# A hybrid decoder step: the mLSTM chunk steps regrouped, decode key gathers in a job of their own, the start's loads reordered

## The chip, the cores and the metric

The kernel runs on one core of a Trainium2 chip. The metric is device time in microseconds for one execution of the whole program; below, TensorE, VectorE, ScalarE, GpSimd and SyncE are PE, DVE, ACT, POOL and SP in the profile's rows, and SP's rows are mostly the DMAs that it issues.

## The reference

One layer of a decoder step, for 1024 prompt tokens (S) and 8 decode tokens (NB), which are handled together as R = 1032 columns of x. What is computed:

```python
h = RMSNorm(x) * norm_w                      # x: 1032 x 2048
aq,ak,av, iq,ik,iw, az, mq,mk,mv, mi,mf, mo,mz = split(h @ w_in)
# prompt attention: the indexer selects the 256 best earlier keys for each query
score[t,s] = sum_h relu(iq[t,h] . ik[s]) * iw[t,h]
att[t]     = softmax over top-256 keys of aq . ak, times av          # 8 heads, 2 KV heads
# decode attention: the same over 4096 cached keys in pages, 256 of them gathered for each of 8 rows
# mLSTM, 4 heads, q and k 128 wide, v 256 wide, chunk by chunk:
s   = (q k^T) * d                            # d = exp(log_d - m_t), causal
num = a * (C q) + s v ;  den = a * (n . q) + sum(s)
h_t = num / max(|den|, exp(-m_t))
C   = a_end * C + sum_s w[s] v[s] k[s]^T ;  n likewise
out = RMSNorm(x + concat(att * silu(az), norm(h_ml) * sigmoid(mo) * silu(mz)) @ w_out)
```

Everything is float32. Outputs are the normed result, the new keys and values, and the mLSTM state for prompt and decode.

## The kernel before, in words

**Projection.** TensorE's main work is h @ w_in, as 61 tiles of up to 128 output columns by 1032 tokens (`proj`, matmuls at L1333). Tile 0 (`T_MISC`, 88 columns) holds the small paths, 1 to 8 are the indexer's queries, then follow k, v and q of attention, q, k and v of mLSTM (25 to 36), the gates of mLSTM (`T_G` = 37 to 52) and of attention (`T_AZ` = 53 to 60). A float32 factor is split into a high and a low part of a type that TensorE takes at full rate (wH, wL by L210 on ScalarE and L211 on VectorE; xH, xL by L261 and L262), and three products replace one: H·H, H·L, L·H. A tile goes in four quarters of four k blocks of 128 rows; with three chunks of 344 tokens a quarter is 4 x 3 x 3 = 36 matmuls. After the fourth quarter `evac` empties the PSUM banks (L329, into `ev` buffers, six in all), scales by the row's rstd, and does what the path needs: for a gate tile a Sigmoid on ScalarE and a product on GpSimd (L371), for tiles below `T_G` a copy of the 8 decode columns into `dec` on GpSimd (L332). After the projection comes the product with w_out (L1470).

**The start.** Tiles 0, 1 and 2 run together, so that x, which is loaded block by block (16 blocks of 128 x 1032, `xr`), is used three times on its arrival. `xbegin` loads block 0 in three chunks and the first quarter of the three tiles' weights, in two parts: k = 0, and k = 1 to 3. `xload(k)` loads each further block, splits it and adds its squares to `acc`. `xhook` calls these ahead of tile 0's matmuls of each quarter. In a quarter the order of weights and x is tile 0's weights, four blocks of x, and then tiles 1 and 2's weights; those of quarter 1 are pinned.

**Lanes.** All else is cut into small pieces placed between the quarters. Two lanes each run a list of jobs; a job is a generator whose `yield` gives a cost. `Lane.step`, called after each quarter, runs pieces until the job's cost is spread evenly up to its due tile. Lane 0: `gates`, `index`, `att` (prompt attention), `ml` (mLSTM of the prompt). Lane 1: `dscore`, `dsel`, `datt` (decode attention), `dml` (mLSTM of decode). A job's line has its first tile, its due tile and its weight:

```python
Job("ml", T_G, T_PRE, 36, job_ml)
```

**Order.** Each engine carries out its instructions in the order that a scheduler gives them; it follows dependences and priorities (weights and evacuations are high), and what is wrapped in `pin` keeps its place in the program's order. SP issues most DMAs, so a load that waits for its buffer holds those behind it in SP's order. Pools give each named tile `bufs` buffers.

**mLSTM steps (`job_ml`).** 16 steps: 8 chunks of 128 tokens by two pairs of heads. For each step `load` fetches q and k (`qk`), v (`vT`, L779) and two rows for each head (`rb`, L783, four DMAs that broadcast a row of `rowS`). `prep` copies the decay's last column (`dk`, L789), forms d = exp of the masked difference on VectorE and ScalarE (L797 is the Exp), scales q, then has on TensorE the scores (L802), with d multiplied at L803, split into dH and dL (`split`, L769 and L770), the transposes of k (L806), scaled and split again (ksH at L769), and those of v, split into aH and aL (L814, L815). `main` does the products: state times q and scores times v (L828 on), the state's update (L832), and the norm of the heads. `tail` transposes the heads (L862, of `hm` from L854) and stores them. The loop runs `main(n)` and the loads of step n + 2, then a quarter of the projection, then `prep(n + 1)` and `tail(n)`, then a quarter. The first `prep` comes three quarters after the first loads.

**Decode attention (`job_datt`).** For each of 8 rows GpSimd gathers 2 x 128 keys by an indirect DMA (`kv`, L1181, a pool of six buffers in the job), two rows ahead of use; VectorE multiplies them by q (`jk`, L1209) and sums. After the softmax the values are gathered in the same way, two rows ahead, and multiplied on TensorE (L1254), eight passes a row, one row to a piece of cost 2500.

**Prompt attention (`job_att`).** At the end of each half of a group's heads the sums of exponentials are transposed, copied into a tile `rt` and stored to `rcS`, which the evacuations of the `T_AZ` tiles read. `rt` takes the single buffer named `ob`, which holds attention outputs too.

Of the kernel before, what the change touches and what calls it, by code (L numbers as in the profile page):

```python
# [8 lines left out]
F32 = mybir.dt.float32  # L9
# [10 lines left out]
NB = 8  # L20
# [117 lines left out]
def body(tc, A, stop=None):  # L138
# [126 lines left out]
    def xbegin():  # L265
        xr = x0.tile([128, R], F32, name="xr")
# [3 lines left out]
        one, rest = slice(0, 1), slice(1, 4)  # L270
        pin(SY.dma_start(nw, A["nw"]))
        for _, _, load, _ in ws:
            pin(load(one, SC))
        pin(SC.activation(warm, mhalf, AF.Square))
        for c in range(3):
            pin(SY.dma_start(xr[:, cs[c]], A["xT"][0, :, cs[c]]))
        for _, _, load, _ in ws:
            pin(load(rest))
        spin(14)
        todo = [lambda c=c: xsplit(0, xr, cs[c]) for c in range(3)]  # L280
        cast = [w[3] for w in ws]
        for f in (lambda: cast[0](one), todo[0], lambda: cast[1](one), lambda: cast[2](one), todo[1], todo[2],
                  lambda: cast[0](rest), lambda: cast[1](rest), lambda: cast[2](rest)):
            a, v = f()
            pin(a)
            pin(v)
        pin(SC.activation(acc, xr, AF.Square))
# [233 lines left out]
    def job_att():  # L521
# [3 lines left out]
        with tc.tile_pool(name="at", bufs=2) as pa:  # L525
# [126 lines left out]
            for n, pair in enumerate(pairs):  # L652
# [103 lines left out]
    def job_ml():  # L756
        gT = mlc["gT"]
        with tc.tile_pool(name="ml", bufs=2) as pm:
# [28 lines left out]
            def prep(c, h0, qk, vT, rb):  # L787
                dk = pm.tile([128, 2], F32, name="dk")
                V.tensor_copy(dk, rb[:, 1, :, 127])  # L789
                d = pm.tile([128, 2, 128], F32, name="d")  # L790

                def col(x):
                    return gT[:, x, h0 * 8 + c:(h0 + 1) * 8 + c + 1:8].unsqueeze(2).to_broadcast([128, 2, 128])

                pin(V.tensor_tensor(d, rb[:, 0], col(0), OP.subtract))
# [3 lines left out]
                V.tensor_tensor(qt, qk[:, 0:2], rb[:, 1], OP.mult)  # L799
                pS = bank().rearrange("p (a b) -> p a b", a=4)  # L800
                for hh in range(2):
                    PE.matmul(pS[:, hh, :], qk[:, 2 + hh, :], qk[:, hh, :], start=True, stop=True)  # L802
                V.tensor_tensor(d, pS[:, 0:2], d, OP.mult)  # L803
                dH, dL = split(d, "d")
                for hh in range(2):
                    PE.transpose(pS[:, 2 + hh, :], qk[:, 2 + hh, :], ident)  # L806
                ks = pm.tile([128, 2, 128], F32, name="ks", bufs=1)
                V.tensor_tensor(ks, pS[:, 2:4], col(1), OP.mult)
                kH, kL = split(ks, "ks")
                pv = bank().rearrange("p (a b) -> p a b", a=2)  # L810
                for x in range(4):
                    PE.transpose(pv[:, x // 2, (x % 2) * 128:(x % 2) * 128 + 128], vT[:, x, :], ident)
                aH, aL = (pm.tile([128, 2, 258], F32R, name=f"a{x}", bufs=1) for x in "HL")
# [54 lines left out]
            ld = [load(*steps[0]), load(*steps[1])]  # L868
            yield 1
            yield 1  # L870
            yield 1
            cur = prep(*ld.pop(0))
            yield 1
            for n in range(len(steps)):
                mid = main(*cur)
                if n + 2 < len(steps):
                    ld.append(load(*steps[n + 2]))
                yield 1
                if n + 1 < len(steps):
                    cur = prep(*ld.pop(0))  # L880
                tail(*mid)
                yield 1
# [186 lines left out]
    def job_dml():  # L1069
        with tc.tile_pool(name="dm", bufs=1, side="right") as pd:  # L1070
# [9 lines left out]
            yield 2000  # L1080
            yield 2000
            yield 2000
# [23 lines left out]
            yield 2000  # L1106
            yield 2000
# [53 lines left out]

    def job_datt():
        with tc.tile_pool(name="da", bufs=1, side="right") as pd:
# [13 lines left out]
            def gather(src, b):  # L1177
                out = []
                for u in range(2):
                    g = pd.tile([128, 256], F32, name="kv", bufs=6)  # L1180
# [3 lines left out]
                    if not u:  # L1184
                        pin(gi)
# [15 lines left out]
            for b in range(NB):  # L1201
                if b + 2 < NB:
                    kgs.append(gather("ck", b + 2))
# [352 lines left out]
```

## Time and profile before

| what | value |
|---|---|
| median of 3 runs | 2077.87 us (2075.32 to 2081.95) |
| the profiled execution | 2064.6 us, its span 2062.8 us |
| PE | 2034.1 us busy, 99% of the span |
| PE weight loads (beside the matmuls) | 1999.7 us, 97% |
| DVE | 1215.2 us, 59% |
| ACT | 836.4 us, 41% |
| POOL | 331.5 us, 16% |
| HBM | 131 GB/s over the span |

The span is that of one profiled execution; its own time is 1.8 us more. A busy TensorE also holds the time in which it runs at a lower clock, so the share alone does not tell how fast it went; the granted clock stands in a row of its own. In rows of waits the columns are the engine and its operation, what released it, the sum of the waits in us, their number, and the longest. In rows of the timeline they are the start, the duration in us, engine, line, operation, and in brackets the idle time ahead and what ended it. In rows by windows they are the window, its length, busy time (and count) of PE, PE weight loads, DVE, ACT and POOL, the granted clock (1 is full), the share of the DMA engines, and GB/s. In rows of groups they are the busy time and the mean in ns, and behind the bar the idle time ahead of them and its releaser.

### The profile page before, as it was taken

How to read it: one execution, taken by the hardware profiler on the slowest of the kernel's cores; microseconds unless marked ns; L12 is line 12 of the kernel's file. 1: busy time of each engine (PE TensorE's matmuls, PEld its weight loads, DVE VectorE, ACT ScalarE, POOL GpSimd, SP SyncE). 2: the span in 40 equal slices, each digit the busy share in tenths (PEclk: the TensorE clock that was granted, in tenths of full speed). 3: DMA queues.
4: the chain of work that ended last, by engine and by line, in shares of the span. 5: the costliest groups of instructions: out<-in, count | busy, mean ns of one | idle time of the engine just before them, and what ended most of it. 6: DMA issues, size and time to landing. Idle time of an engine off the chain costs nothing.

```text
span 2062.8 us, 36440 instructions
## 1 busy us (share of the span) xinstructions
PE 2034.1 (99%) x13284; PEld 1999.7 (97%) x13284; DVE 1215.2 (59%) x3060; ACT 836.4 (41%) x1667; POOL 331.5 (16%) x405
## 2 busy tenths in 40 slices
PE   8999999999999999999999999989999999999997
PEld 8999999999999999999999999989999999999997
DVE  8332457556695876886455455356676467374464
ACT  8122244233531455312365555434454235343343
POOL 0002556600000000024011001012222111101011
PEclk9999999999999999999999999999999999999998
DMA  7444533322222212254322332256665758586584
GB/s 244 106 110 116 157 108 113 107 75 72 78 68 74 72 59 71 63 168 136 107 75 86 107 98 70 72 158 190 189 198 161 190 194 273 150 249 182 148 256 138
DMA packets 229777, 272.85 MB, mean 132 GB/s; under 512 B 36661, under 2 KB 162741, under 8 KB 229597
## 3 DMA queue, kind: packets, MB, share of 16 engines
q1 hardware_dynamic: 222381, 256.70, 42.0%
q0 software_dynamic: 5632, 12.59, 2.2%
q8 instruction: 104, 1.70, 0.4%
q10 hardware_dynamic: 1584, 1.23, 0.2%
q14 instruction: 76, 0.62, 0.1%
HBM read 210.54 MB, written 59.88 MB: 131 GB/s over the span
## 4 chain that ended last, share of the span: by engine, by line
PE 88%; DMA 4%; DVE 3%; ACT 1%; issue 1%; SPq 1%; POOL 0%; DVEq 0%; ACTq 0%; POOLq 0%
PE pj L1333 56%; PE bank L1470 17%; PE bank L441 3%; PE bank L636 2%; PE bank L585 2%; PE bank L627 2%; PE bank L935 1%; PE bank L1333 1%; DMA qk<-mlS 1%; DMA xr<-in_xT_dram 1%; DMA ev<-gateS 0%; DMA out_C_s_dram<-Cb 0%; PE bank L1053 0%; DVE wL L211 0%; DMA rb<-rowS 0%
## 5 line engine op out<-in xcount | busy, mean ns | idle before, releaser
L1333 PE MATMUL pj<-xH,wH 128*128 128x344 f32 (+2 forms) x2736 | 883.5, 324 | 6.3 <-ACT xH L261 3.2
L1333 PE MATMUL pj<-xL,wH 128*128 128x344 f32 (+2 forms) x2736 | 883.2, 323 | 0.2 <-DVE xL L262 0.2
L1333 PE MATMUL pj<-xH,wL 128*128 128x344 f32 (+2 forms) x2736 | 882.9, 323 | 0.0
L210 ACT CAST wH<-wraw 128x512 fp32r<-128x512 f32 (+2 forms) x439 | 267.6, 614 | 636.1 <-PE pj L1333 429.4
L1333 PEld LDWEIGHTS pj<-xH,wH 128*128 128x128 f32 (+1 forms) x2736 | 513.5, 188 | 10.6 <-ACT xH L261 4.8
L1333 PEld LDWEIGHTS pj<-xL,wH 128*128 128x128 f32 (+1 forms) x2736 | 513.4, 188 | 3.0 <-DVE xL L262 1.0
L1333 PEld LDWEIGHTS pj<-xH,wL 128*128 128x128 f32 (+1 forms) x2736 | 513.9, 188 | 2.0
L211 DVE TENSOR_TENSOR wL<-wraw,wH 128x512 fp32r<-128x512 f32 (+2 forms) x439 | 305.5, 700 | 350.6 <-ACT wH L210 338.3
L1470 PE MATMUL bank<-mH,wH 128*128 128x388 f32 (+1 forms) x768 | 245.0, 321 | 0.4 <-ACT wH L210 0.4
L1470 PE MATMUL bank<-mL,wH 128*128 128x388 f32 (+1 forms) x768 | 244.9, 319 | 0.0
L1470 PE MATMUL bank<-mH,wL 128*128 128x388 f32 (+1 forms) x768 | 244.4, 319 | 0.0
L922 POOL DMA_INDIRECT kp<-in_cik_dram,idx x128 | 128.6, 1005 | 105.6 <-PE bank L935 56.3
L1470 PEld LDWEIGHTS bank<-mH,wH 128*128 128x128 f32 x768 | 144.3, 188 | 0.7 <-ACT wH L210 0.6
L1470 PEld LDWEIGHTS bank<-mL,wH 128*128 128x128 f32 x768 | 144.5, 188 | 0.0
L1470 PEld LDWEIGHTS bank<-mH,wL 128*128 128x128 f32 x768 | 144.2, 188 | 0.0
L490 ACT ACTIVATE eq<-eq 128x512 bf16<-128x512 bf16 (+2 forms) x93 | 78.4, 843 | 113.7 <-DVE eq L489 113.4
L443 ACT ACTIVATE rl<-bank 128x512 f32<-128x512 f32 (+2 forms) x160 | 79.0, 522 | 79.5 <-PE bank L441 51.9
L446 DVE SCALAR_TENSOR_TENSOR s<-rl,wiN,s 128x512 f32<-128x512 f32 (+2 forms) x150 | 94.9, 654 | 21.5 <-ACT rl L443 18.4
L329 DVE TENSOR_TENSOR ev<-pj,rstd 128x344 f32<-128x344 f32 x144 | 73.6, 512 | 53.7 <-PE pj L1333 44.9
L632 DVE TENSOR_TENSOR ptL<-bank,ptH 128x512 fp32r<-128x512 f32 (+1 forms) x80 | 50.5, 635 | 64.3 <-ACT ptH L631 63.7
L1480 POOL TENSOR_TENSOR acc<-acc,sq 128x388 f32<-128x388 f32 (+1 forms) x42 | 43.1, 1025 | 280.3 <-ACT sq L1478 280.3
L332 POOL COPY dec<-ev 128x8 f32<-128x8 f32 x28 | 11.4, 406 | 475.9 <-DVE ev L329 198.9
(367 smaller groups left out, 2441.6 us busy)
## 6 DMA issues: line engine op xcount, KB each, us to landing
wraw<-in_wa_dram SPq DMA_DIRECT2D x238, 256.0 KB
wraw<-in_wo_dram SPq DMA_DIRECT2D x192, 256.0 KB
gateS<-ev SPq DMA_DIRECT2D x72, 172.0 KB
mlS<-ev SPq DMA_DIRECT2D x48, 172.0 KB
xr<-in_xT_dram SPq DMA_DIRECT2D x15, 516.0 KB
mL<-gateS SPq DMA_DIRECT2D x32, 194.0 KB
xr<-in_xT_dram SPq DMA_DIRECT2D x32, 194.0 KB
out_yT_dram<-y SPq DMA_DIRECT2D x32, 194.0 KB
```

What stands on the lines that cost most here:

```text
L210: a = SC.copy(H[:, s, :cols], raw[:, s, :cols])
L211: return a, V.tensor_tensor(L[:, s, :cols], raw[:, s, :cols], H[:, s, :cols].bitcast(F32), OP.subtract)
L329: V.tensor_tensor(e, ps[c][:cols, :cn], rstd[:cols, c0:c0 + cn], OP.mult)
L441: PE.matmul(p[:, :cn], qi[:, h % 4, :], ki[x][:, c0:c0 + cn], start=(x == 0), stop=(x == 1))
L443: SC.activation(r[:, :cn], p[:, :cn], AF.Relu)
L446: v = V.scalar_tensor_tensor(s[:, c0:c0 + cn], r[:, :cn], wv, s[:, c0:c0 + cn], OP.mult, OP.add)
L490: SC.activation(junk2[:, :W1], junk2[:, :W1], AF.Copy, accum_out=cnt[:, 1:2])
L632: V.tensor_tensor(pL[:, :kw], pt[:, :kw], pH[:, :kw].bitcast(F32), OP.subtract)
L922: g = G.indirect_dma_start(out=kp, out_offset=None, in_=A["cik"], in_offset=bass.IndirectOffsetOnAxis(ap=idx[:, m:m + 1], axis=0))
L1333: PE.matmul(ps[:cols, :cn], w_[:, k, :cols], x_[kk][:, c0:c0 + cn], start=(kk == 0 and z == 0), stop=(kk == 15 and z == 2))
L1470: PE.matmul(p, w_[:, k, :], x_, start=(n == 0), stop=(n == 47))
L1480: G.tensor_tensor(acc, acc, sq, OP.add)
```

## The change

Four parts; the projection, the indexer and the output product stay.

- **mLSTM steps.** `prep` is cut in two: `decay` (dk, d, Exp, scaled q) and `prep` (the three kinds of TensorE work first, the splits behind them). `decay` of a step runs one step ahead of its `prep`, loads run three steps ahead, the first `prep` comes after five quarters of waiting, and `tail(n)` moves to the piece after `prep(n + 1)`, ahead of `main(n + 1)`. `dk` is pinned. `dml` waits one piece longer at two places.
- **Decode gathers.** The gathers of keys go into a job `rows` of lane 1 ahead of `datt`, with a pool of 16 buffers; those of the values follow one row behind the use of the keys. A row of value products costs 1500 in place of 2500.
- **Attention's row sums** are copied into a buffer of the six named `pP` and no longer into `ob`.
- **The start.** Weights of quarter 0 come in three parts (k = 0, k = 1, k = 2 and 3), x of k = 1 is loaded ahead of the second part and split by `xbegin`; of the later loads of x only k = 2 is pinned; for quarter 1 tile 0's weights are pinned, and those of tiles 1 and 2 are not.

The due tile of `att` goes from 48 to 47.75 and some weights follow.

```diff
 def xbegin():
-        xr = x0.tile([128, R], F32, name="xr")
+        xr = [x0.tile([128, R], F32, name="xr") for k in range(2)]
...
-        one, rest = slice(0, 1), slice(1, 4)
+        parts = slice(0, 1), slice(1, 2), slice(2, 4)
...
+        pin(SY.dma_start(xr[1], A["xT"][1]))
+        for s in parts[1:]:
+            for w in ws:
+                pin(w[2](s))
         spin(14)
...
+        both(xsplit(0, xr[0], cs[2]))
+        for w in ws:
+            both(w[3](parts[1]))
+        both(xsplit(1, xr[1], slice(0, R)))
+        add(0, acc)
+        for w in ws:
+            both(w[3](parts[2]))
+        add(1, x0.tile([128, R], F32, name="sq", bufs=2))
...
 def xload(k):
-        if k < 4:
+        if k == 2:
             pin(dma)
...
 # job_att
-                    rt = pa.tile([128, 2, 128], F32, name="ob", bufs=1)[:32, 0]
+                    rt = pa.tile([128, 512], F32, name="pP", bufs=6)[:32, :128]
...
 # job_ml
-            def prep(c, h0, qk, vT, rb):
+            def decay(c, h0, qk, vT, rb):
                 dk = pm.tile([128, 2], F32, name="dk")
-                V.tensor_copy(dk, rb[:, 1, :, 127])
+                pin(V.tensor_copy(dk, rb[:, 1, :, 127]))
...
+                return c, h0, qk, vT, dk, d, qt
+
+            def prep(c, h0, qk, vT, dk, d, qt):
...
             ld = [load(*steps[0]), load(*steps[1])]
+            for _ in range(5):
+                yield 1
+            dcs = [decay(*ld.pop(0))]
             yield 1
+            cur = prep(*dcs.pop())
+            ld.append(load(*steps[2]))
+            dcs = [decay(*ld.pop(0))]
             yield 1
-            yield 1
-            cur = prep(*ld.pop(0))
-            yield 1
+            mid = None
             for n in range(len(steps)):
+                if mid:
+                    tail(*mid)
                 mid = main(*cur)
-                if n + 2 < len(steps):
-                    ld.append(load(*steps[n + 2]))
+                if n + 3 < len(steps):
+                    ld.append(load(*steps[n + 3]))
                 yield 1
                 if n + 1 < len(steps):
-                    cur = prep(*ld.pop(0))
-                tail(*mid)
-                yield 1
+                    cur = prep(*dcs.pop())
+                    if n + 2 < len(steps):
+                        dcs = [decay(*ld.pop(0))]
+                    yield 1
+            tail(*mid)
...
+    def job_rows():
+        rowctx.pool = rowctx.enter_context(tc.tile_pool(name="kvp", bufs=1, side="right"))
+        yield 1
+        for b in range(NB):
+            kgs.append(gather("ck", b))
+            yield 1
...
 # job_datt
             for b in range(NB):
-                if b + 2 < NB:
-                    kgs.append(gather("ck", b + 2))
+                if b:
+                    vgs.append(gather("cv", b - 1))
...
-            vgs = [gather("cv", b) for b in range(2)]
+            vgs.append(gather("cv", NB - 1))
...
-                if b + 2 < NB:
-                    vgs.append(gather("cv", b + 2))
...
-                yield 2500
+                yield 1500
...
+                   Job("rows", T_AK, 35.5, NB + 1, job_rows),
...
 # proj, xhook
-                        ws.append(wsplit(wsrc(t, q), cols, x0, 2, 4, q == 1))
+                        ws.append(wsplit(wsrc(t, q), cols, x0, 2, 4))
...
-            ws.append(wsplit(wsrc(0, q), NMISC, wst, 2, 3, q == 1))
+            ws.append(wsplit(wsrc(0, q), NMISC, wst, 2, 3, True))
...
-        for k in range(max(1, q * 4), q * 4 + 4):
+        for k in range(max(2, q * 4), q * 4 + 4):
             xload(k)
```

More of the change, by code (lines that the diff above doesn't have):

```diff
@@ L1176, in job_datt @@
             lT = pd.tile([128, 2, 64], F32, name="lT")
[L1177 to L1180, printed above, removed]
-                    gi = G.indirect_dma_start(out=g, out_offset=None, in_=A[src],
-                                         in_offset=bass.IndirectOffsetOnAxis(ap=idxs[:, b, u:u + 1], axis=0))
-                    out.append(g)
-                    if not u:
-                        pin(gi)
-                return out
             def qload(b):
```

78 lines of the change are left out of this document (46 added, 32 removed).

## The prediction

> **What bounds the kernel now.** The page comes first: spans and busy shares by engine, then the granted clock by slice.
>
> ```profile
> span 2062.8 us, 36440 instructions
> ...
> PE 2034.1 (99%) x13284; PEld 1999.7 (97%) x13284; DVE 1215.2 (59%) x3060; ACT 836.4 (41%) x1667; POOL 331.5 (16%) x405
> ...
> PEclk9999999999999999999999999999999999999998
> ```
>
> TensorE is busy for 2034.1 of 2062.8 us. The change removes and adds no matmul: the built programs hold the same number of each kind. So it can only move what TensorE loses: 28.7 us of idle time, and stretches at a lower clock, which count as busy. The second view is the list of waits, for PE alone: in total, times, the longest.
>
> ```profile
> PE pj L1333 <- ACT xH L261: 3.2, 3, 1.5
> PE bank L806 <- DVE d L803: 2.7, 2, 2.6
> PE pj L1333 <- DVE ev L329: 2.4, 2, 1.6
> PE bank L862 <- DVE hm L854: 2.0, 2, 1.1
> ...
> PE bank L1333 <- ACT wH L210: 0.8, 1, 0.8
> ...
> PE bank L832 <- ACT ksH L769: 0.6, 1, 0.6
> PE bank L1254 <- DMA kv<-in_cv_dram,idxs: 0.5, 2, 0.4
> ```
>
> L261 and L210 belong to the start, L806, L862 and L832 to the mLSTM steps, L1254 to decode attention; L329 is the evacuation of a projection tile. These 12.2 us are all that the change can aim at, beside clock losses.
>
> The third view is the timeline at these places, with one row of the chain that ended last as the yardstick, and the clock by windows.
>
> ```profile
> 1614.32 66.34 PE pj L1333 x422
> ```
>
> An undisturbed projection matmul takes 66.34 / 422 = 0.157 us.
>
> ```profile
> 977.04:980.45 3.41, 2.88 (x21) 2.31 (x20) 0.00 (x0) 0.00 (x0) 2.78 (x3) 1.00 0.41 124
> 980.50:983.90 3.40, 3.40 (x14) 3.40 (x14) 0.00 (x0) 0.47 (x1) 1.91 (x3) 0.53 0.33 92
> 1349.20:1352.60 3.40, 0.84 (x7) 0.67 (x6) 1.93 (x6) 0.69 (x2) 0.99 (x2) 1.00 0.25 30
> 1352.70:1355.80 3.10, 3.10 (x13) 3.10 (x13) 1.37 (x5) 0.34 (x2) 0.00 (x0) 0.51 0.94 263
> 981.14 0.49 PE L1333 MATMUL pj<-xL,wH 128*128 128x344 f32 x1
> ...
> 983.72 0.49 PE L1333 MATMUL pj<-xL,wH 128*128 128x344 f32 x1
> ```
>
> The column after the POOL count is the granted clock. It stood at 0.53 and 0.51 in two stretches of some 3.4 us, each behind a stretch of that length in which PE did little. Between the last two rows nine matmuls start in 2.58 us, 0.287 each instead of 0.157. Eleven in such a stretch: 11 x 0.130 = 1.4 us lost, twice.
>
> **The change part by part.** Working is against the profiled execution: 2064.6 us, its span and 1.8 around it. The median of the three runs, 2077.87, lies 13.3 us above; I take that as constant and subtract the same microseconds from it.
>
> *The start.* Three places:
>
> ```profile
> 4.89 0.65 ACT L210 CAST wH<-wraw 128x128 fp32r<-128x128 f32 x2
> ...
> 9.85 1.15 ACT L261 ACTIVATE xH<-xr,nw 128x1032 fp32r<-128x1032 f32 x1 [0.89 <-DMA xr<-in_xT_dram]
> 11.05 0.70 PE L1333 MATMUL pj<-xH,wH 128*88 128x344 f32 x3 [1.52 <-ACT xH L261]
> 27.35 0.70 PE L1333 MATMUL pj<-xH,wH 128*88 128x344 f32 x3 [0.90 <-ACT xH L261]
> 28.81 0.44 PE L1333 MATMUL bank<-xH,wH 128*128 128x388 f32 x1 [0.76 <-ACT wH L210]
> 4.00:8.00 4.00, 2.95 (x16) 2.07 (x15) 2.89 (x8) 3.31 (x9) 0.00 (x0) 1.00 1.04 319
> ```
>
> At 9.85 ScalarE waits for x of k = 1, which was queued behind three quarters of the first weights. The change queues it ahead of them, and puts a k = 1 part of 176 KB before the rest. So 352 KB less (three quarters of 704 KB make 528; 176 stay) lie ahead of k = 1's work; at 319 GB/s of the last row that is 1.1 us. The wait of 1.52 falls to 0.4. The casts of that part (three of 0.65 / 2, some 0.3 us) then run in ScalarE's idle 0.89. At 27.35 and 28.81 TensorE had nothing but the 88-column tile for k = 4 to 7: the other two tiles' second weights were issued behind x of k = 7. In the changed program's SP order both stand ahead of x of k = 4, and PE's order takes 21 matmuls for each k instead of 9, so 21 x 0.157 = 3.3 us cover each x load. Of 0.90 + 0.76 = 1.66 I take 1.2 away. Together -2.3; at best -3.2. The bound on the other side: the Square of x0 now stands behind the split of x1 (1.15 us), and x3's load waits for that buffer: +1.2.
>
> *Attention's row sums in another buffer.* Two copies at the end of a head group no longer wait for the ob buffer. No wait for them is in the list of PE; the transposed sums go to DRAM and are read tiles later. Nothing; were they late, their reader is the gate stage, some 30 us on.
>
> *Decode attention.* Key gathers go ahead of it, in a job of their own, on 16 buffers instead of 6, and value gathers follow one batch row behind, so GpSimd stops waiting for VectorE there:
>
> ```profile
> POOL kv L1181 <- DVE jk L1209: 32.6, 16, 3.0
> 917.39 0.39 PE L1333 MATMUL pj<-xH,wH 128*128 128x344 f32 x1 [0.76 <-DVE ev L329]
> 969.75 2.73 PE L1254 MATMUL bank<-PT,kv 128*128 128x4 f32 x24
> ```
>
> The wait at 917.39 is an evacuation behind jk work; that work keeps its size, so I count half: -0.4. Gathers queued on GpSimd wait for the index list; behind them stand the dec copies, which hold one evacuation buffer of six, used by three chunks a tile: covered. The value matmuls (L1254) lose the wait of 0.5 for gathers, and the slow stretch after 980.5 (1.4): -1.9. But with all values there, the changed order holds all 64 passes without a projection matmul among them. At 2.73 / 24 = 0.114 us that is 7.3 us in which the array streams four columns at a time. The 24 of before brought no lower clock; the mixed stretch from 977.04, with PE at 2.88 of 3.41, did. Bounds: nothing, or half the clock from 3.4 us on: 3.9 us of passes become 7.8, and 1.4 are lost behind them: +5.3. I take half, 2.6, nearest to the row from 977.04. Net +0.7; with the evacuation, +0.3.
>
> [...]
>
> *The mLSTM steps.*
>
> ```profile
> 1333.71 0.50 SPq L783 DMA_DIRECT2D rb<-rowS  x1
> ...
> 1335.68 0.90 SPq L783 DMA_DIRECT2D rb<-rowS  x2
> ...
> 1341.62 0.34 DVE L789 COPY dk<-rb 128x2 f32<-128x2 f32 x1 [5.50 <-DMA rb<-rowS]
> 1343.10 0.43 PE L1333 MATMUL pj<-xH,wH 128*128 128x344 f32 x1 [1.64 <-DVE ev L329]
> 1350.67 0.17 DVE L789 COPY dk<-rb 128x2 f32<-128x2 f32 x1 [5.59 <-DMA rb<-rowS]
> 1351.93 0.44 PE L806 MATMUL bank<-cst,qk 128*128 128x128 f32 x2 [2.56 <-DVE d L803]
> ...
> 1345.00:1600.00 255.00, 249.63 (x1660) 245.79 (x1659) 166.07 (x561) 116.10 (x250) 55.71 (x102) 0.99 0.63 178
> ```
>
> VectorE, in order, stands 5.5 us at a row load, twice; the evacuation behind the first, and the score product d behind the second, hold TensorE. The change loads three steps ahead, gives five quarters (of 36 matmuls, 5.7 us) instead of three before the first, and takes decay a step ahead of its products. SP issued the first step's four rb rows from 1333.7 to 1336.6, two quarters before use; with two quarters more, 11 us, these waits end. The transposes of k stand before d now, so L806's wait cannot occur. Heads are transposed (L862) after two quarters and the products between them, not one and some: 2.0 goes. L832's 0.6 came of the late d. Sum: 1.6 + 2.7 + 2.0 + 0.6 + 1.4 of clock = 8.3. The gates of decode's mLSTM share VectorE in the first steps, and a first wait for rb may stay: I take -7.0; from -8.3 to -2.
>
> The price: the order has 62 activation table loads, not 46, as Exp of decay falls between the Sigmoids of gates.
>
> ```profile
> L797 ACT ACT_TABLE_LOAD x8 | 10.3, 1283 | 0.3 <-DMA gateS<-ev 0.2
> L803 DVE TENSOR_TENSOR d<-bank,d 128x256 f32<-128x256 f32 x16 | 6.7, 419 | 7.4 <-PE bank L802 7.4
> L769 ACT CAST dH<-d 128x256 fp32r<-128x256 f32 x16 | 6.5, 406 | 11.8 <-DVE d L803 11.8
> L770 DVE TENSOR_TENSOR dL<-d,dH 128x256 fp32r<-128x256 f32 x16 | 6.9, 430 | 0.0
> L815 DVE TENSOR_TENSOR aL<-bank,aH 128x512 fp32r<-128x512 f32 x16 | 11.0, 684 | 0.3
> L211 DVE TENSOR_TENSOR wL<-wraw,wH 128x512 fp32r<-128x512 f32 x35 | 26.5, 757 | 18.3 <-ACT wH L210 16.1 <-DMA gateS<-ev 2.2
> L329 DVE TENSOR_TENSOR ev<-pj,rstd 128x344 f32<-128x344 f32 x24 | 12.1, 508 | 7.9 <-POOL ev L371 4.3 <-PE pj L1333 3.5
> ```
>
> 16 x 1.283 = 20.5 us of ScalarE. Cover: between a step's transposes and its products lie 36 matmuls, 5.7 us. The chain in them is d 0.42, dH 0.41, dL 0.43, the same three for the keys, and aL 0.68: 3.2 us, with one weight split (0.76) 4.0. One load more makes 5.2, below 5.7. So hidden; for places where an evacuation joins, +0.5, up to +17 (below).
>
> **Sum.** -2.3 + 0.3 - 7.0 + 0.5 = -8.5. Profiled: 2056.1; median: 2069.4.
>
> **Rivals.** *Clock and start* (2074): the value batch costs its full 5.3, so decode gives +5.3 - 1.9 - 0.4 = +3.0, and the start gives back what it gains, because loads are the bound there (DMA share 1.04 in its row). 0 + 3.0 - 7.0 + 0.5 = -3.5. For it: the two clock rows; against: the 24 passes at full clock.
>
> *The waits only move* (2074): VectorE still meets rows that have not landed, as SP queues them between weight loads that wait for buffers; the first steps keep 6 of 8.3 us. -2.3 + 0.3 - 2.3 + 0.5 = -3.8. That the program is not what the edit says is excluded by its order: 36 matmuls stand between every two parts.
>
> *Table loads in the steps* (2085): where a gate's evacuations fall into the cover, the chain is 4.0 + three evacuations (1.5) + a load (1.3) = 6.8, 1.1 us over 5.7; with 0.3 for the evacuation behind, TensorE loses 1.4. In 12 of 16 steps that is 16.8: -2.3 + 0.3 - 7.0 + 16.8 = +7.8. It decides from 11 steps on (15.4 - 9.0 = +6.4). For it: ScalarE's order puts Exp between two Sigmoids of one tile. Against: of before's waits in such steps the list has none for aL or kL, and evacuations come once in four quarters.
>
> **Chances.** Forecast case 0.66, clock and start 0.13, waits move 0.10, table loads 0.11. A measurement of this kernel can tell some 0.3%, 6 us, about the spread of its three runs. Faster takes in the forecast case down to -6.2, 0.62 in all; the rest of it and the two small gains are the same: 0.27; table loads slower: 0.11. The range goes from all gains at best (start -3.2, decode -0.8 - 1.9, mLSTM -8.3: -14.2, some 2063.5, so 2063) to no change and a little, 2080, which takes in both small rivals; above it lies the table case, below it little.
>
> **What would show it.** In the changed profile: L261 and L210 gone from PE's waits before 30 us; no dk wait over 1 us; PE idle between 1345 and 1600 under 1.5 us instead of 255.0 - 249.6 = 5.4; granted clock below 1 only around the 64 passes. Wrong would be: PE waiting for aH, dL or ksH in many steps, evacuations late by more than 1 us in the gate stage, or a slow clock elsewhere.

## The result, and the profile after

The changed kernel takes 2084.70 us (median of 20 runs, 2083.11 to 2090.55), the kernel before beside it 2079.59 us (20 runs, 2074.26 to 2087.15): a ratio of 1.0029, 95% interval 1.0020 to 1.0037. By the ratio it is slower by some 6 us (5.1 us by the medians), where 8.5 us less had been forecast.

The page of the changed kernel, its span and the busy shares:

```profile
span 2086.0 us, 36465 instructions
...
PE 2045.0 (98%) x13284; PEld 2007.8 (96%) x13284; DVE 1212.2 (58%) x3063; ACT 859.4 (41%) x1686; POOL 332.8 (16%) x405
```

TensorE has the same 13284 rows. Beside the first profile of before it is busy for 10.9 us more (2045.0 against 2034.1) and idle for 41.0 us instead of 28.7. But that profile is of an execution of 2064.6 us, and beside the changed kernel before takes 2079.59 us. Nearer to that is the third profile of before (under Experiments), of an execution of 2077.55 us and a span of 2075.7 us:

```profile
PE 2037.4 (98%) x13284; PEld 1999.6 (96%) x13284; DVE 1214.7 (59%) x3060; ACT 837.1 (40%) x1667; POOL 330.0 (16%) x405
```

Against it the changed kernel's span is 10.3 us longer: PE is busy for 7.6 us more, at a mean granted clock of 0.992 instead of 0.996, and idle for 2.7 us more. So most of the loss is a lower clock. The waits of PE in the changed kernel (total, times, longest):

```profile
PE pj L1369 <- DVE ev L346: 7.7, 6, 2.7
PE pj L1369 <- DVE gi L1117: 7.7, 1, 7.7
...
PE bank L251 <- DVE rstd L253: 1.6, 2, 0.8
...
PE pj L1369 <- ACT xH L261: 1.1, 2, 0.7
```

The lines have moved by some 36: L1369 is the projection, L346 the evacuation. Of the waits of before, those for d, hm, ksH, wH and the value gathers are gone, and 1.1 us for xH is left. In their place stand one of 7.7 us behind gi, which is decode's mLSTM, and more late evacuations. Where the clock went is in the timeline and in the windows:

```profile
10.77 0.49 PE L1369 MATMUL pj<-xL,wH 128*88 128x344 f32 x1
11.05 0.49 PE L1369 MATMUL pj<-xH,wL 128*88 128x344 f32 x1
...
988.93 10.25 PE L1289 MATMUL bank<-PT,kv 128*128 128x4 f32 x64
...
989.00:992.60 3.60, 3.60 (x35) 3.60 (x33) 0.69 (x1) 0.01 (x1) 1.43 (x2) 1.00 0.25 76
992.80:1002.80 10.00, 10.00 (x43) 10.00 (x44) 0.27 (x1) 0.00 (x0) 0.00 (x0) 0.50 0.08 13
1364.80:1371.40 6.60, 3.50 (x12) 3.53 (x13) 1.96 (x8) 6.48 (x9) 0.94 (x2) 0.50 0.44 124
```

At 11 us projection matmuls start 0.28 us apart, not 0.157, though the row of 8 to 12 us has the granted clock at 1.00; at 72 us, where they have 388 columns, 0.33, not 0.18 as from 74.7 us on, and the row of 72 to 76 us has 0.69. Both are about half the rate. The 64 value passes take 10.25 us, not 7.3; from 3.8 us behind their start to 1002.8 us the clock is at 0.50, though PE is never idle there. The third window lies around the end of the longest stall, and has the clock at 0.50 too.

The mLSTM steps begin at 1345 us. Around the 7.7 us, SP, VectorE, ScalarE and PE did this:

```profile
1356.58 0.43 SPq L1099 DMA_DIRECT2D gi<-miscS  x1
...
1357.60 0.50 SPq L1102 DMA_DIRECT2D bb<-in_bg_dram  x1
...
1354.19 0.43 DVE L815 TENSOR_TENSOR qt<-qk,rb 128x256 f32<-128x256 f32 x1 [8.41 <-DMA rb<-rowS]
...
1359.24 0.42 DVE L815 TENSOR_TENSOR qt<-qk,rb 128x256 f32<-128x256 f32 x1 [4.02 <-DMA rb<-rowS]
1363.19 0.23 DVE L1109 TENSOR_TENSOR gi<-gi,bb 128x64 f32<-128x64 f32 x1 [3.52 <-DMA bb<-in_bg_dram]
...
1366.80 0.19 DVE L1116 SCALAR_TENSOR_TENSOR gi<-gi,w 128x32 f32<-128x32 f32 x1 [2.16 <-ACT w L1115]
...
1367.25 0.51 DVE L346 TENSOR_TENSOR ev<-pj,rstd 128x344 f32<-128x344 f32 x1
...
1363.71 1.28 ACT L1114 ACT_TABLE_LOAD   x1 [8.86 <-DVE w L1113]
...
1365.25 1.28 ACT L1115 ACT_TABLE_LOAD   x1
...
1367.90 0.62 PE L1369 MATMUL pj<-xH,wH 128*128 128x344 f32 x1 [7.67 <-DVE gi L1117]
```

VectorE stands 8.4 us and 4.0 us at qt for rb, then at gi for a load that SP issued at 1357.6, then 2.2 us for an Exp and a logarithm with a table load each. The evacuation at 1367.25, which PE needed from 1360 on, is behind all of them. (PE's row names gi, which ends at the same moment.)

### The profile page after: what moved, and what is told of

The parts are those of the page before. It is cut to its first block, busy times and chain, and to the rows that moved or that the text cites. A ratio compares the mean times of both kernels' runs of the same rounds, so it can differ in the third digit from the quotient of the medians.

```text
span 2086.0 us, 36465 instructions
## 1 busy us (share of the span) xinstructions
PE 2045.0 (98%) x13284; PEld 2007.8 (96%) x13284; DVE 1212.2 (58%) x3063; ACT 859.4 (41%) x1686; POOL 332.8 (16%) x405
## 4 chain that ended last, share of the span: by engine, by line
PE 88%; issue 3%; DVE 3%; another core or an unknown queue 2%; DMA 2%; ACT 1%; SPq 1%; POOL 0%; DVEq 0%; ACTq 0%; POOLq 0%
PE pj L1369 55%; PE bank L1506 17%; PE bank L458 3%; PE bank L653 2%; PE bank L602 2%; PE bank L1369 2%; PE bank L644 1%; PE bank L962 1%; PE bank L845 1%; PE bank L851 1%; PE bank L847 1%; PE bank L1289 0%; PE bank L1080 0%; DVE wL L211 0%
## 5 line engine op out<-in xcount | busy, mean ns | idle before, releaser
L1369 PE MATMUL pj<-xH,wH 128*128 128x344 f32 (+2 forms) x2736 | 886.1, 325 | 18.5 <-DVE ev L346 7.7
L1369 PE MATMUL pj<-xL,wH 128*128 128x344 f32 (+2 forms) x2736 | 883.2, 323 | 1.1 <-issue 1.0
L1369 PE MATMUL pj<-xH,wL 128*128 128x344 f32 (+2 forms) x2736 | 882.2, 323 | 0.8 <-issue 0.6
L1369 PEld LDWEIGHTS pj<-xH,wH 128*128 128x128 f32 (+1 forms) x2736 | 514.7, 188 | 25.0 <-issue 13.0
L1369 PEld LDWEIGHTS pj<-xL,wH 128*128 128x128 f32 (+1 forms) x2736 | 514.4, 188 | 4.0 <-issue 1.6
L1369 PEld LDWEIGHTS pj<-xH,wL 128*128 128x128 f32 (+1 forms) x2736 | 514.7, 188 | 3.5 <-issue 1.3
L346 DVE TENSOR_TENSOR ev<-pj,rstd 128x344 f32<-128x344 f32 x144 | 73.8, 512 | 75.7 <-PE pj L1369 47.3
```

The source lines that it names most:

```text
L346: V.tensor_tensor(e, ps[c][:cols, :cn], rstd[:cols, c0:c0 + cn], OP.mult)
L1369: PE.matmul(ps[:cols, :cn], w_[:, k, :cols], x_[kk][:, c0:c0 + cn], start=(kk == 0 and z == 0), stop=(kk == 15 and z == 2))
```

## Experiments

Ratios are against the kernel before in the same comparison. The runs came in four comparisons, on chips that the record numbers 14, 1, 14 and 7, and before takes 2063, 2083, 2079 and 2079 us in them, so a time is compared only with times beside it.

### Before, profiled again

The kernel unchanged, twice.

> The kernel before, unchanged, profiled once more and timed against itself. Between 218 and 430 us the changed kernel's trace has PE stalls of 13 us (four evacuations late by 0.6 to 2.9 us, and waits that end with nothing that the profile shows), though every engine's order of instructions is the same there in both kernels; the trace of before has none. Theory A: these stalls come to either kernel in most executions, and the profiled execution of before (2064.6 us) was an undisturbed one. Then this trace shows over 5 us of such stalls in that stretch, and a span of 2070 to 2080 us. Theory B: the change causes them. Then this trace has under 2 us there and a span below 2067 us. Ratio 1.000 by both.

> The kernel before, profiled a third time. Its two profiles so far come from executions near 2063 us and have no PE stall between 218 and 430 us, while the changed kernel's profiles, from executions on a chip where before takes 2079 to 2083 us, lose 13 to 21 us there. If before's runs beside this one are above 2075 us, theory A (that stretch is slow on such a chip with either kernel) expects 13 to 21 us of PE loss there in this trace too; theory B (only the changed kernel loses there) expects under 2 us, and its loss elsewhere. If before's runs are near 2063 us, both expect under 2 us and the changed kernel beside it tells.

The second profile of before, in the first comparison: 2062.89 against 2063.11 us, ratio 1.000 (0.9991 to 1.0009). The third profile, in the fourth: 2078.08 against 2078.79 us, 1.000 (0.9991 to 1.0009). The stretch from 215 to 435 us by windows, in the changed kernel, and in the second and the third profile of before:

```profile
215.00:435.00 220.00, 209.85 (x1362) 203.84 (x1361) 119.77 (x314) 69.56 (x168) 115.07 (x121) 1.00 0.39 114
```

```profile
215.00:435.00 220.00, 220.00 (x1454) 218.65 (x1455) 129.75 (x332) 74.48 (x183) 114.60 (x120) 1.00 0.39 119
```

```profile
215.00:435.00 220.00, 210.14 (x1372) 205.77 (x1372) 122.14 (x318) 69.63 (x170) 113.85 (x119) 1.00 0.38 113
```

PE is idle for 10.2 us there in the changed kernel, not at all in before where it takes 2063 us, and for 9.9 us in before where it takes 2078. The second profile came out as its theory B had it (no stall, a span of 2060.9 us), the third as its theory A: the stall comes with the comparison, and not with the change. What makes the difference between comparisons stays open; the chip's number does not settle it, as number 14 stands at 2063 us and at 2079 us. The same stretch has 9.9 of the 12.9 us between the first and third span of before, and so most likely most of the 13.3 us by which before's median lay above its profiled execution.

### The three parts alone

```diff
 # e2: job_ml, dml's pieces and due times only
 # e3: xbegin, xload, xhook, wsplit of quarter 1 only
 # e4: job_rows, gathers of datt, value rows of 1500 only
```

> The kernel before with only the mLSTM part of the change (decay apart from prep, tail later, loads three steps ahead, dml's extra pieces, the due times). In the traces the mLSTM stretch (1300 to 1550 us) lost 10.9 us of PE time before and 9.4 us after, since one stall of 8.1 us behind gi, with 1.5 us of half clock, has taken the place of the old ones. Theory A (the wait moved): ratio 0.999 to 1.000, that is 0 to -2 us, and a trace with one PE stall of 5 to 9 us behind an evacuation that stands behind gi or qt on VectorE. Rival, the prediction's step: -7 us, ratio 0.9966, no such stall.

> The kernel before with only the start part of the change. The changed trace lost 5.1 us in the first 50 us where before lost 6.0, because the matmuls from 4.6 to 12.6 us ran at 0.29 each, half the clock, and 3.4 us from 50 to 100 us where before lost 1.1. Theory A: the reordered loads do not let the clock rise after the warm-up matmuls, so half clock until 12 us is seen here too; ratio 1.000 to 1.001. Rival, the prediction's step: -2.3 us, ratio 0.9989, with the matmuls of the first 10 us 0.16 apart.

> The kernel before with only the decode attention part (key gathers in a job of their own, 16 buffers, value gathers one row behind, value rows of 1500). In the traces the stretch from 900 to 1050 us lost 4.8 us before and 8.9 after: an evacuation late by 2.9 us at 935 and half clock behind the 64 value passes. Theory A: +3 to +5 us, ratio 1.0015 to 1.0025, with the late evacuation and the slow clock both in the trace. Rival, the prediction's step: +0.3 us, ratio 1.000.

Against before at 2063.11 us: mLSTM 2058.23 us, 0.9978 (0.9969 to 0.9987); start 2064.33 us, 1.0010 (1.0001 to 1.0019); decode attention 2071.78 us, 1.0044 (1.0030 to 1.0058). By the ratios -4.5, +2.1 and +9.1 us, together +6.6: the change's 6 us are about the sum of its parts, and the decode part carries them. mLSTM lies between the two theories, the start at theory A's upper end, decode on theory A's side at twice its size.

In mLSTM alone the longest stall in the steps is 2.4 us, an evacuation behind dk, and no wait of PE there is behind gi. VectorE still comes to dk right behind the first loads and waits for rb about as long as before; the added quarters are in the program and not in VectorE's order:

```profile
1341.10 0.85 DVE L792 COPY dk<-rb 128x2 f32<-128x2 f32 x1 [5.15 <-DMA rb<-rowS]
```

Decode alone, a late evacuation, the value passes, two projection matmuls after, and the clock beneath the passes:

```profile
919.72 0.40 PE L1343 MATMUL pj<-xH,wH 128*128 128x344 f32 x1 [2.37 <-DVE ev L329]
...
973.00 10.81 PE L1263 MATMUL bank<-PT,kv 128*128 128x4 f32 x64
...
984.38 0.49 PE L1343 MATMUL pj<-xH,wH 128*128 128x344 f32 x1
984.67 0.49 PE L1343 MATMUL pj<-xL,wH 128*128 128x344 f32 x1
...
978.20:981.60 3.40, 3.40 (x18) 3.40 (x17) 0.00 (x0) 0.00 (x0) 0.00 (x0) 0.50 0.00 0
```

10.81 - 7.3 = 3.5 us in the passes, and 20 projection matmuls at 0.287 behind them, 20 x 0.13 = 2.6: 6.1 us of clock. But before has a slow stretch in this place as well. The stage in before, profiled again, and in decode alone:

```profile
960.00:1000.00 40.00, 39.64 (x254) 38.11 (x253) 10.30 (x26) 9.45 (x16) 15.45 (x16) 0.96 0.48 145
```

```profile
960.00:1000.00 40.00, 40.00 (x227) 38.85 (x227) 13.81 (x38) 10.47 (x17) 5.85 (x6) 0.83 0.35 107
```

0.04 x 40 = 1.6 us of clock are lost in the one and 0.17 x 40 = 6.8 in the other: 5.2 more. The evacuation's wait goes from 0.3 to 2.4: 2.1 more. That is 7.3 of the 9.1 us. In these two profiles the rest stands in the first 60 us, where the orders of the two kernels are the same (313 matmuls against 329): luck of the execution.

VectorE's first work of datt waits 5.1 us for the index stage's last store, 1.7 in before, and the products of keys then run into the tile's end:

```profile
DVE c L1168 <- DMA biasS<-gt: 1.7, 1, 1.7
```

```profile
DVE c L1190 <- DMA biasS<-gt: 5.1, 1, 5.1
```

Of before (first row) and decode alone. The store was issued at 896.30 us in before and at 897.98 in decode alone, and the wait ended 2.2 and 5.0 us later; from 896 to 899 us the DMA share was 0.76 and 0.94, as the key gathers now run at the same time. That they delay the store is likely by this and was not tried apart.

For the start, against before profiled again: less idle time of PE from 4 to 60 us (1.2 us against 1.8), and 0.8 us more of it from 60 to 76 us, at the rstd of the rows. In eight profiles with the old start PE was busy for 51.8 to 54.2 us of the first window and 14.54 of the second in each; in ten with the new one for 54.3 to 55.3 and 13.75 or 13.76. The slow rate until 11 or 12 us came with either start, in some profiles and not in others, so theory A's size, no gain, holds, but its reason does not. Up to 900 us PE is idle for 4.3 us in before and for 4.4 in start alone. What start alone loses comes later, in prompt attention (before, profiled again, and start alone):

```profile
1100.00:1300.00 200.00, 200.00 (x1370) 196.76 (x1369) 103.09 (x338) 111.39 (x253) 17.92 (x18) 1.00 0.30 90
```

```profile
1100.00:1300.00 200.00, 197.44 (x1337) 193.49 (x1336) 101.09 (x333) 121.81 (x257) 17.97 (x18) 0.99 0.30 90
```

PE is idle for 2.6 us there, 1.6 of it for ptH, the softmax weights that ScalarE splits. The edit touches nothing in that stage; but ScalarE's order has 60 table loads in this kernel instead of 46, and 24 instead of 13 in this stretch. Whether these make the wait was not tried.

### The value passes apart

```diff
 # e9: in datt's value loop, on the changed kernel
+                pt = pd.tile([128, 2, 8], F32, name="ptb", bufs=1)
+                V.tensor_copy(pt, PT[:, 0:2, b * 8:b * 8 + 8])
-  ... PT[:, u, o:o + 4] ...
+  ... pt[:, u, v * 4:v * 4 + 4] ...
```

> The changed kernel, unchanged, profiled again beside the other three. The parts alone measured, against before, 0.9978 (mLSTM), 1.0010 (start) and 1.0044 (decode attention): -4.6, +2.1 and +9.1 us by their ratios, together +6.6. Theory A (the parts add, and the stalls of 13 us between 218 and 430 us in the changed kernel's first trace belong to that execution): ratio 1.002 to 1.004, a span near 2068 us, PE stalls between 218 and 430 us under 2 us. Theory B (the parts together cause stalls that none has alone): those stalls are here again, 10 us or more, and the span is over 2078 us.

> The changed kernel with the 64 value passes in eight groups of 8 and 21 projection matmuls between them (each row's weights are copied into one small buffer, so the next row's copy waits for the row before), with nothing pinned. Changed kernel: ratio 1.0024 to 1.0031, its 64 passes took 10.2 to 10.8 us and were followed by 12 to 20 projection matmuls at 0.287. Theory A (a long run of narrow passes halves the clock): the passes take 7.2 us in all, no matmul near them is 0.287 apart, 4 to 6 us are gained, ratio 1.000 to 1.001. Rival (the narrow passes cost the same in any arrangement, or the gaps between rows cost as much): gain under 2 us, ratio over 1.002.

The changed kernel again: 2090.32 against 2082.97 us, 1.0031 (1.0021 to 1.0040), with 13.3 us of stalls from 215 to 435 us. So theory B's signs came, but not its reason: the third profile of before has such stalls too, and no part alone had them because the parts ran in the comparison at 2063 us. The ratio is as theory A had it. Rows apart: 2079.91 against 2078.87 us, 1.0005 (0.9996 to 1.0014): by the two ratios 5.4 us gained, theory A. Its passes, the clock over all eight groups, and a late evacuation:

```profile
988.52 0.95 PE L1291 MATMUL bank<-ptb,kv 128*128 128x4 f32 x8
...
992.72 0.95 PE L1291 MATMUL bank<-ptb,kv 128*128 128x4 f32 x8
...
988.50:1019.00 30.50, 30.50 (x215) 30.50 (x214) 6.37 (x16) 3.96 (x7) 1.24 (x1) 1.00 0.19 59
...
933.36 0.40 PE L1371 MATMUL pj<-xH,wH 128*128 128x344 f32 x1 [3.34 <-DVE ev L346]
```

Eight passes and 21 projection matmuls in turn keep the clock at 1.00. The late evacuation stays. Another run had pinned values and projection matmuls in place:

> The changed kernel with the value products of decode attention pinned among the projection matmuls, so that PE's order has 16, 24 and 24 passes with 36 projection matmuls between, in place of 64 in one run. Nothing else of the change is altered. In the trace of decode alone the 64 passes took 10.81 us (7.2 at the full rate) and 20 projection matmuls behind them started 0.287 apart. Theory A (the clock halves because of 7 us of narrow passes): no slow stretch there, 5 to 6 us less than the changed kernel on the same chip. Rival (the slow clock comes of the waits or of something else at that place): the stretch stays and the gain is under 2 us.

2113.37 us, 1.0151: the pins moved the transposes of the scores ahead of their data, PE stood 11.3 us for them, and one group of 24 passes (990.59 to 993.18 us) was still followed by a clock of 0.51. It answers nothing on the gain.

```profile
PE bank L1258 <- issue: 11.3, 1, 11.3
...
994.40:997.80 3.40, 3.40 (x14) 3.40 (x13) 0.00 (x0) 0.00 (x0) 0.00 (x0) 0.51 0.00 0
```

On the kernel before, with the decode part alone, rows apart gained nothing:

> The kernel before with the decode attention part alone and the value rows apart. The decode part alone gave 1.0044 (+8.7 us by the medians); the rows apart took 1.0030 of the changed kernel to 1.0005. Theory A (the run of 64 narrow passes is the main term, the evacuation late behind the keys' products the second): ratio 1.001 to 1.0025, with a late evacuation of 2 to 3.5 us near 920 us left. Rival (the values are all of it): ratio 0.999 to 1.0005 and no such evacuation.

2094.76 against 2078.79 us, 1.0078 (1.0061 to 1.0094), more than the 1.0044 of decode alone. Both theories missed. The clock is 1.00 around the passes here too. The late evacuation is there (3.0), but most is new waits in the mLSTM steps, in their old form:

```profile
PE pj L1345 <- DVE ev L329: 5.1, 4, 3.0
PE bank L862 <- DVE hm L854: 4.8, 3, 2.0
PE bank L812 <- DVE C L834: 4.1, 2, 3.3
```

C waited there for a qt whose qk came 6.9 us late. Why the old steps fall apart when decode attention ends later was not tried; the new steps bear the same edit better (rows apart, above), though PE waits 2.3 us for a dH there.

### What stands in front of the evacuation at 1367 us

```diff
 # e7: on the changed kernel
+                pin(V.tensor_tensor(qt, qk[:, 0:2], rb[:, 1], OP.mult))
 # e8: on the changed kernel
-            for _ in range(4):
+            for _ in range(12):
                 yield 2000          # job_dml, ahead of gi
...
-  ... T_PRE - 0.5, 20000 + 16 * 2500 + 5000, job_dml ...   # the job's weight
+  ... T_PRE - 0.5, 36000 + 16 * 2500 + 5000, job_dml ...
```

> The changed kernel with one more pin: the scaled q (qt, L815), which VectorE's order had put two quarters ahead of dk and d, where it stood 8.4 and 4.0 us for rb, keeps its place behind d. In the changed trace the evacuation at 1367 us then came 7.7 us late, behind qt and behind dml's gates (gi, whose loads SP issued at 1356 to 1358). Theory A (the hoisted qt is what makes VectorE late): that stall is under 2 us and the time falls by 6 to 8 us against the changed kernel on the same chip. Rival B (gi decides, since it waits for its own load, and an Exp and a Log with a table load each follow before the evacuation): the stall stays within 2 us of its size and the time within 2 us.

> The changed kernel with decode's mLSTM (dml) waiting 12 pieces in place of 4 before its first work on the gates (gi), so that it no longer falls into the first mLSTM steps; qt is not pinned. Theory A (the hoisted qt decides): the stall before the evacuation near 1367 us stays at 4 us or more, the time falls by under 3 us. Rival B (gi and its two table loads decide): the stall goes below 2 us and the half clock behind it too, and the time falls by 7 to 9 us against the changed kernel on the same chip.

Beside the changed kernel's 1.0031: qt pinned 2086.62 us, 1.0011 (1.0000 to 1.0021); gates later 2084.05 us, 1.0004 (0.9993 to 1.0014). PE's row at that place in the changed kernel profiled again, with qt pinned, and with the gates later:

```profile
1370.78 0.63 PE L1369 MATMUL pj<-xH,wH 128*128 128x344 f32 x1 [5.92 <-DVE gi L1117]
```

```profile
1367.50 0.62 PE L1369 MATMUL pj<-xH,wH 128*128 128x344 f32 x1 [5.37 <-DVE gi L1117]
```

```profile
1361.84 0.40 PE L1369 MATMUL pj<-xH,wH 128*128 128x344 f32 x1 [0.39 <-DVE ev L346]
...
1368.24 0.43 PE L1369 MATMUL pj<-xH,wH 128*128 128x344 f32 x1 [2.37 <-DVE ev L346]
```

Without the early qt the stall is nearly the same, since gi's own load ends last: so far rival B. But qt pinned gained 4 us, which neither theory has. Most of that is not of the edit. PE up to 1335 us, where every engine's order is the same in the two kernels, in the changed kernel profiled again and with qt pinned:

```profile
0.00:1335.00 1335.00, 1311.32 (x8522) 1278.82 (x8523) 787.02 (x2042) 541.31 (x1088) 209.83 (x232) 0.99 0.33 99
```

```profile
0.00:1335.00 1335.00, 1315.62 (x8544) 1281.60 (x8545) 788.55 (x2045) 543.89 (x1091) 212.55 (x232) 0.99 0.33 99
```

22 matmuls, some 3 us, of the 4.3 us between the two profiles are there already. With gi later the stall falls to 0.4, another of 2.4 comes one tile on, and by the ratios 5.6 us are gained, short of rival B's 7 to 9. A part of this may be luck of the same kind (8549 matmuls by 1335 us); in the steps themselves, from 1335 to 1640 us, PE is idle for 3.8 us instead of 5.9, and the half clock behind the stall is gone.

A repair by force, gate evacuations pinned ahead of qt and gi:

> The changed kernel with the evacuations of the gate tiles pinned, so that VectorE's order has the first qt and gi behind an evacuation that is due and not ahead of it: their waits for loads then fall into the middle of a tile. Theory A (what was lost at 1367 us is a wait for late loads that stands ahead of an evacuation, whoever waits): no PE stall over 2 us between 1340 and 1400 us, a gain of 6 to 9 us, ratio 0.999 to 1.000. Rival (the work of gi and its table loads has to be paid somewhere, and moves the stall to another evacuation): a stall of 4 us or more in the next tile, ratio over 1.002.

> The kernel before with the mLSTM part alone, and the evacuations of the gate tiles pinned as in the run before. The mLSTM part alone gave 0.9978 with stalls of 2.7 us (evacuation behind dk, which waited 5.15 us for rb), 0.9 and 1.7 us left. Theory A: the first goes, ratio 0.9955 to 0.9970 (-6 to -9 us), what the prediction had put on this part (-7). Rival (another wait takes its place): ratio 0.9975 to 0.9990.

> The changed kernel with both repairs, value rows apart and evacuations of the gate tiles pinned. If the two places add: 10 to 14 us below the changed kernel, ratio 0.996 to 0.998. If the clock or the late evacuations come back at other places: ratio over 0.999.

2159.13 us (1.039), 2155.97 us (1.0364), 2172.57 us (1.0453) against 2078.87 us. All three are far above what theory A, or the sum, had for them. The rivals of the first and the third (over 1.002, over 0.999) came true in direction only; the second's range is missed too. The first of them:

```profile
PE pj L1371 <- DVE ev L346: 23.1, 12, 5.0
PE bank L883 <- DVE hm L875: 12.9, 3, 4.5
```

Pinned instructions keep their order among themselves. In its trace three evacuations stand in one row at 1606.8 us, behind dk, d and the products of decode's state, and hm waits in other tiles: the stall moved into many places. The pins reach beyond the gate tiles: near 967 us PE stands 10.2 us at the transposes of decode's scores.

### The mLSTM part with the gates later, and two repairs

> The kernel before with the mLSTM part alone and decode's mLSTM waiting 12 pieces in place of 4 before its gates. mLSTM alone gave 0.9978. In the changed kernel the same delay took 0.0027 off the ratio. Theory A (gi and its table loads meet the first steps here too): 0.996 to 0.9972. Rival (alone, the stalls left are dk's 2.7 us behind rb, which this does not touch): 0.9973 to 0.9983.

> The changed kernel with value rows apart, dml's gates 12 pieces later and qt pinned. By the single repairs (1.0031 to 1.0005 by the value rows, 1.0031 to 1.0004 by the gates) the sum would be 0.9978 to 0.9985. If the waits move to other evacuations: over 0.9995.

Against before at 2078.79 us: 2072.68 us, 0.9965 (0.9953 to 0.9976), and 2075.69 us, 0.9986 (0.9977 to 0.9995). The first lies in theory A's range, the second a ten-thousandth above its sum's. The first is the fastest version: the kernel before with the mLSTM part and 12 pieces ahead of gi, 7.3 us faster than before by the ratio. That the later gates make it faster than mLSTM alone (0.9978) is not shown: the two intervals overlap, mLSTM alone has no wait of PE behind gi, and the evacuation behind dk, of which the rival spoke, is still late, by 1.9 us. PE's busy time from 1335 to 1600 us in before profiled again, the changed kernel, mLSTM alone, and mLSTM with the gates later:

```profile
1335.00:1600.00 265.00, 257.69 (x1713) 253.57 (x1712) 171.35 (x568) 119.22 (x253) 59.61 (x106) 0.99 0.62 177
```

```profile
1335.00:1600.00 265.00, 257.33 (x1708) 255.31 (x1707) 157.55 (x537) 125.09 (x247) 47.83 (x94) 0.99 0.62 176
```

```profile
1335.00:1600.00 265.00, 260.32 (x1742) 257.44 (x1741) 168.98 (x569) 129.34 (x262) 58.73 (x106) 1.00 0.62 180
```

```profile
1335.00:1600.00 265.00, 261.07 (x1736) 258.17 (x1735) 161.59 (x536) 123.96 (x249) 51.52 (x98) 0.99 0.60 176
```

Idle 7.3, 7.7, 4.7 and 3.9 us: in the changed kernel the steps' gain is eaten by one wait, of 7.67 us.

## Why the prediction was wrong

- **The decode part: the term that was most mis-sized** (+0.3 forecast, +9.1 measured, 6 to 12). The 64 passes were seen in the changed order and bounded at 0 to +5.3; half was taken. They cost 6.1 us, and the 1.4 us of the old slow stretch were taken off rightly. Two rows should have decided it. "The 24 of before brought no lower clock" spoke for 2.7 us of passes, not for 7.3. And the first of the two clock rows was misread: "PE did little" does not fit 2.88 us busy of 3.41. That stretch held 14 narrow passes and two short waits, together 0.53 us, and the clock behind it was 0.53: this row spoke rather for the full bound. Half the clock from 3.4 us on was the author's estimate, by the 3.41 and 3.40 us of the stretches ahead of the two slow ones; in the changed kernel it was 3.8 us, and the clock was 0.50 with PE busy for 10.00 of 10.00 us. No run shows the 2.6 us that were taken: decode alone showed the 6.1. Rows apart, in which nothing is pinned and the clock stays at 1.00 for 30.50 us, show that the unbroken run of passes is the cause of the clock loss. The evacuation behind the products of keys was to lose half of its 0.76; it grew to 2.4, behind a longer wait of datt's first work for the index stage's store, at which the prediction had not looked.
- **The mLSTM part: another wait in the place of the old ones** (-7.0 forecast, -4.5 alone, 2.7 to 6.4). The waits for d, hm and ksH went as said. The step that failed is "with two quarters more, these waits end": the extra quarters were counted in the program, while VectorE's order put dk (in mLSTM alone, 5.15 us of wait and an evacuation 2.4 us late) or qt and dml's gi (in the changed kernel, 7.67 us) ahead of an evacuation. "No dk wait over 1 us" came true in the changed kernel and meant nothing, as qt waited in dk's stead; PE's idle time from 1345 to 1600 us was 7.7 us, not under 1.5. The rival "the waits only move" names this.
- **The start** (-2.3 forecast, +2.1 measured, 0.2 to 3.9). The waits were those of one execution: xH cost 3.2 us in the first profile of before and 1.0 in the second, in which PE ran slowly until 11 us and did not wait at that place at all. Those at 27 and 28 us went, 0.8 us came at the row sums, and by 900 us nothing was gained or lost. The loss that was measured lies in prompt attention, in which the prediction looked for no cost; its cause stays open.
- **Table loads** (+0.5): PE has no wait for aH, dL or ksH in the changed kernel, as forecast. But the reason given for 62 loads in place of 46 fails: the Exp of decay has 12 instead of 8, and start alone, with the old steps, has 60, decode alone 58, mLSTM alone 54. Any of the parts reorders ScalarE. The two loads in front of the evacuation at 1367 us are decode's Exp and logarithm; in before that Exp needs no load, so one of 1.28 us is new there.
- **Row sums:** no wait for them is in the changed kernel's list. **The constant of 13.3 us** held: before takes 2079.59 us beside the changed kernel, and shows the same stalls where its time is high.
- **The chances:** the rivals stood as alternatives, each with the other terms at their forecast. Clock, start and moved waits came together, as nothing forbade; a case with all three (start 0, decode +3.0, mLSTM -2.3, table loads +0.5) would have been +1.2, near no change.

## What to carry to other kernels

In this kernel, whose TensorE is busy for 99% of the span before and 98% after, 64 small matmuls in one run cost 6.1 us of clock (decode alone): spread such a batch among wide ones, and look at what the spreading moves (here it gained 5.4 us with the new steps and nothing with the old ones). Room given in the program (more pieces, earlier loads) is worth only what the order on each engine keeps of it, so read where every instruction with a load behind it stands against the next evacuation, those of the neighbouring job too. Here it paid to delay the instruction that waits; pinning the evacuations that suffer cost some 74 us against the changed kernel, for one stall of 6 us. And take a wait of one profile for the kernel's only when a second profile has it.

## What the runs showed of the hardware

TensorE's clock fell to 0.50 with no idle time at all, under 64 passes of four columns in one run: in the changed kernel 3.8 us behind the first of them, with PE busy for all of the 13.87 us from the first to 1002.80 us; in decode alone the passes start at 973.00 us, and from 978.20 to 981.60 us the clock is 0.50 with PE busy for 3.40 of 3.40 us. Eight at a time with 21 matmuls of 344 columns between left it at 1.00 over 30.50 us (rows apart). Runs of 24 passes, 2.6 us, were followed by the half clock in some profiles (0.51 above, and in the mLSTM part with the gates later, below) and not in others (before, 1.00 from 972.40 to 976.00 us behind the passes from 969.75):

```profile
990.20:993.60 3.40, 3.40 (x14) 3.40 (x14) 0.47 (x1) 0.00 (x0) 2.60 (x3) 0.50 0.61 171
```

One kernel took 2063 us in one comparison and 2078 to 2083 us in others, with 10 us of the difference as idle time of PE in one stretch of 220 us, in which decode's index keys are gathered and the order of every engine is the same.

The type of the split factors is the faster one in TensorE: in before a product of 128x258 takes 0.12 us in it (L828, starts at 1388.12 and 1388.24 us) and 0.44 us in plain float32 (L826, two records: 0.56 us from their start at 1387.56 to 1388.12 us, less one L828 of 0.12 in between).
